# The sample's second SwiGLU on an unnormalised residual held in accumulators, and single banks for the last down products

## The chip, the core and the metric

The kernel runs on one core of one Trainium2 chip. A core has five engines that run on their own and wait for each other by semaphores: TensorE (PE in the profile, its weight loads PEld), VectorE (DVE), ScalarE (ACT), GpSimd (POOL) and SyncE (SP), which here issues nearly all DMAs. The metric is the device time of one launch in microseconds; lower is better. The time before is a median of 2969.23 us.

## What is computed

A two-layer encoder trunk with a residual stream of width 1024, for two request groups with the same weights: a prompt of 1024 tokens and a sample of 512. Layer 0 mixes tokens by a grouped Fourier transform, layer 1 by grouped-query attention; after each comes a dense SwiGLU with 2816 hidden columns.

```python
def rms_norm(x, g):
    y = xf * lax.rsqrt(jnp.mean(xf * xf, axis=-1, keepdims=True) + EPS)
    return (y * g.astype(jnp.float32)).astype(x.dtype)

def swiglu_ffn(x, g, w_gate, w_up, w_down):
    h = rms_norm(x, g)
    return (jax.nn.silu(h @ w_gate) * (h @ w_up)) @ w_down

for i in range(DEPTH):
    x = x + (fourier_mixer if i % 2 == 0 else attention_mixer)(x, ...)
    x = x + swiglu_ffn(x, norm_ffn[i], ...)
```

Since the norm's factor `rsqrt(mean(x*x) + EPS)` is one number per token, `(r*x*g) @ w` equals `r * ((x*g) @ w)`: the factor may be put on a product's result.

## The kernel before

Tokens lie along the free dimension in blocks of 512: block 0 is the sample, blocks 1 and 2 are the prompt. A residual is eight tiles of 128 features by 512 tokens. Every float32 operand is split into a high and a low part (`split`, L238: ACT writes the high part, DVE or POOL the low one), and every product is three matmuls (`mm3`, L249 to L251).

Two streams are written as Python generators and interleaved by `weave`. Each `yield` states an estimated cost, and the stream with the least stated cost so far goes on. A scheduler then sets each engine's order; a later instruction can be put ahead where it does not depend on what stands before. Each engine executes in its order and waits at the head.

The sample's stream, `main_1`, is attention's projections (`qkv(0)`), its attention, the output projection (`out_projection`, `linear_residual`), `prepare`, and the second SwiGLU (`ffn(1, 0, ...)`). It runs beside `aux_2`, the prompt's projections, attention, output projection and the preparation (`moving`) of the prompt's second SwiGLU. That one (`ffn_pair`) follows alone and fills the last 600 us; it treats the prompt's two blocks together by a scheme with seven products for eight.

Around the change:
- `linear_residual` loads the old residual into a temporary `x`, adds the product, and gives it to `new_residual`. That stores it to DRAM (`xres`, L332), squares it, and sums the squares in `ss`. After the last tile `rstd_cols` (L308) sums over features on PE, and `rsqrt` makes the factor on DVE.
- `prepare(0, 1)` runs `normed`: `in_rows` (L316, L317) spreads the factor over the partitions on PE, each residual tile is reloaded (L366), multiplied by it (L369) and by the gain, and split into `h` (L245, L246).
- `ffn` goes through 22 chunks of 128 hidden columns. A chunk has a gate chain and an up chain of 24 matmuls each into two banks `ga`, `up` (tiles `g`, of which there are two), then Silu (L851), product (L852) and split. The down products (`c<-mid`) of two chunks are added to eight accumulators. The accumulators are 4 buffers in all, two for a block, and attention's transposed tiles (`pt`) rotate through those that are free. For the sample's first SwiGLU (`here`) the residual already stands in accumulators, and the factor `first["r"]` is multiplied onto `ga` and `up` (L849, L850); for its second the accumulators are loaded from `xres`.
- `attend` treats 128 query rows at a time: `scores` (tile `g` or `a`, row maxima L1346, Exp L1350, scaling L1352), `turned` (transposes L1364, split into `pt`), and after each second block `values`. The prompt's scores have one buffer of two banks.
- `product` in `ffn_pair` is one down product: three matmuls into `chain[d]` and a DVE add to an accumulator (L1054). A chain of products sums in its bank, and each partial sum is added to an accumulator. In all rounds but the last the four chains have single banks (tiles `c` and `g`); in the last they share two tiles of two banks each (`a`, of the pool that also takes the pair's gate and up sums). The output of a finished tile is sent at L329.

Of the kernel before, what the change touches and what calls it, by code (L numbers as in the profile page):

```python
# [10 lines left out]
F32 = mybir.dt.float32  # L11
# [3 lines left out]
ALU = mybir.AluOpType  # L15
# [4 lines left out]
NC = D // P  # L20
TB = 512
# [5 lines left out]
NF = DFF // P  # L27
# [98 lines left out]
def trunk_kernel(ctx: ExitStack, tc: tile.TileContext, t: dict):  # L126
# [59 lines left out]
    def tmp(n=TB, dt=F32):  # L186
        return tl("t", [n], dt, "t" + cur[0])
# [66 lines left out]
    nxt, first = {}, {}  # L254
# [71 lines left out]
    def new_residual(b, dc, piece, out=None, stays=False, room=None, later=None, ends=(0, NC - 1)):  # L326

        if out is not None:
            sp.dma_start(out, piece)  # L329
            return  # L330
        if not stays:
            sp.dma_start(xres[b][:, dc, :], piece)  # L332
        if dc == ends[0]:
            ss[b] = later if later is not None else room() if room else tl("ss", [TB], F32, "ss" + cur[0])
            act.activation(ss[b], piece, AF.Square)
        else:
            sq = room() if room else side()
            act.activation(sq, piece, AF.Square)
            dve.tensor_tensor(ss[b], sq, ss[b], op=ALU.add)
        if dc == ends[1]:  # L340
            rstd[b] = cp.tile([P, 4], F32, name=nm("rs"))
            if later is not None:
                whole_sums.append(b)
            else:
                rstd_cols(rstd[b], ss.pop(b), D)
# [398 lines left out]
    def linear_residual(src, u, b, prev):  # L744

        for n in range(NC):
            w = weights(src[n])
            x = tmp()
            sp.dma_start(x, prev[:, n, :])
            ps = bank()  # L750
            project(w, u, ps)
            dve.tensor_tensor(x, ps, x, op=ALU.add)
            new_residual(b, n, x)
            yield 5.5


    kept, pend = {}, []

    def ffn(layer, b, h, out=None):
        h = h()  # L760
        here = b in resident
        acc = resident.pop(b) if here else accumulators()
        kept[b] = acc
        yield 0.0

        def halves(ms, wds, f0, dc):

            box = []

            def half(i):  # L770
                w = wds[dc // 4].rearrange("p h (f c) n -> p h f c n", f=2)
                mm3(box[0], w[:, 0, i, dc % 4], w[:, 1, i, dc % 4], ms[i][:, 0], ms[i][:, 1], i == 0, i == 1)

            def begin():
                box.append(bank())
                if f0 == 0 and not here:
                    sp.dma_start(acc[dc], xres[b][:, dc, :])
                half(0)

            def end():  # L780
                half(1)
                dve.tensor_tensor(acc[dc], box[0], acc[dc], op=ALU.add)  # L782
                if f0 + 2 == NF:
                    new_residual(b, dc, acc[dc], None if out is None else out[:, dc, :])

            return begin, end

        def one(n=1):
            for _ in range(n):
                if pend:  # L790
                    pend.pop(0)()

        ready = {v: first[i] for i, v in enumerate((("gate", 0), ("up", 0), ("gate", 1)))} if here else {}

        def want(v, fc):
            if fc < NF and (v, fc) not in ready:
                ready[v, fc] = weights(down_src(layer, fc, "AB".index(v)) if v in "AB" else t[v][layer, fc])

        def open_items(ms, f0):

            wds = [ready.pop(("A", f0))]
            pairs = [halves(ms, wds, f0, dc) for dc in range(NC)]
            turns = [pairs[0][0], pairs[1][0], pairs[0][1], pairs[1][1]]
            for v in pairs[2:]:
                turns.extend(v)
            pend.extend(turns)
            return wds

        wds = None
        want("gate", 0)  # L810
        want("up", 0)
        for fc in range(NF):
            f0, odd_ = fc - fc % 2, fc % 2
            wg, wu = ready.pop(("gate", fc)), ready.pop(("up", fc))
            if not odd_ and wds is not None:
                want("B", f0 - 2)
                wds.append(ready.pop(("B", f0 - 2)))
            ga, up = bankg(), bankg()
            for dc in range(NC):
                if odd_ and dc == 4:  # L820
                    want("A", f0)
                part(wg, h, ga, dc)
                if here and fc == 0:
                    part(wu, h, up, dc)
                if not odd_ and dc >= 5:
                    one()
                if dc % 2:
                    yield 1.36 if odd_ or dc < 5 else 2.0 if dc == 5 else 2.7
            if odd_:
                want("gate", fc + 1)  # L830
                wds = open_items(ms, f0)
            for dc in range(NC):
                if not odd_ and dc == 3:
                    want("gate", fc + 1)
                if fc == NF - 1 and dc == 4:
                    want("B", f0)
                if dc == (2 if odd_ else 4):
                    want("up", fc + 1)
                if not (here and fc == 0):
                    part(wu, h, up, dc)  # L840
                if not odd_:
                    one(2 if dc in (2, 4, 6) else 1)
                elif dc >= 6:
                    one()
                if dc % 2:
                    yield (3.4 if dc > 1 else 2.7) if not odd_ else 2.7 if dc == 7 else 1.36
            s = tmp()
            if here:
                dve.tensor_tensor(ga, ga, first["r"], op=ALU.mult)  # L849
                dve.tensor_tensor(up, up, first["r"], op=ALU.mult)  # L850
            act.activation(s, ga, AF.Silu)  # L851
            dve.tensor_tensor(up, up, s, op=ALU.mult)  # L852
            m = tl("mid", [2, TB], F32R, "mid")
            split(m[:, 0], m[:, 1], up)
            if odd_:
                ms.append(m)
            else:
                ms = [m]
        want("B", NF - 2)
        wds.append(ready.pop(("B", NF - 2)))  # L860
# [61 lines left out]
    def ffn_pair(layer, blocks, ring, places, outs):  # L922
# [111 lines left out]
        def product(k, d, f0):  # L1034

            name, m, (o, c) = CHAINS[k]
            if f0 == 0 and d == 0 and k < 3:
                load_acc(*((blocks[1], 0), (blocks[1], 1), (blocks[0], 1))[k])
            if d == 0 and k % 2 == 0 and k < 6:
                next(preps[0])  # L1040
            if k == 6 and d == 3:
                preps.pop(0)
            b, dc = blocks[c], 4 * o + d
            acc = accs[b][dc]
            fresh, closes = k in (0, 4, 6), k in (3, 5, 6)
            if fresh and f0 + 2 < NF:
                chain[d] = bank() if d % 2 else bankg()
            elif fresh and d % 2 == 0:
                g2 = tl("a", [2, TB], F32, "gT", gt)
                chain[d], chain[d + 1] = g2[:, 0], g2[:, 1]  # L1050
            x, wd = spots[m], ops[name][:, :, d * P : (d + 1) * P]
            read[m] -= 1
            mm3(chain[d], wd[:, 0], wd[:, 1], x[:, 0], x[:, 1], fresh, True, skip_group_check=True)
            dve.tensor_tensor(acc, chain[d], acc, op=ALU.add)  # L1054
            if f0 + 2 == NF and LAST[o, c] == name:
                new_residual(b, dc, acc, None if outs is None else outs[b][:, dc, :], room=spare, later=sums_of(b, dc), ends=(4, 3))
# [248 lines left out]
    def attend(blocks, straight, slot):  # L1305
# [6 lines left out]
        for g in range(NKV):  # L1312
# [15 lines left out]
            for h in range(g * GROUP, (g + 1) * GROUP):  # L1328
# [49 lines left out]
                    act.copy(o, po[:, 0:256])  # L1378
                    sp.dma_start(dot[blocks[n]][:, h, c0 : c0 + 256], o)

                last = None
                for qc in range(nk + 1):
                    p = scores(qc) if qc < nk else None
                    yield 0.7 * nb
                    if qc:
                        turned(qc - 1, last)
                        yield 0.8 * nb
                        if qc % 2 == 0:
                            values(qc // 2 - 1)
                            yield 0.8 * nb  # L1390
                    last = p


    def weave(main, main_cost, aux=None, aux_cost=1.0, lead=0):
# [11 lines left out]
                runs.remove(run)  # L1406
        cur[0] = "F"

    FFN_US, PAIR_US, CHAIN_US, PROMPT_US = 352.0, 678.0, 223.0, 630.0

    mpt = open_pool("mp")
# [60 lines left out]

    def prepare(b, layer):

        yield from normed(b, g_ffn[layer], nxt, "A")

    def h_next():
        return nxt["h"]
# [62 lines left out]
    def main_1():  # L1541
        yield from qkv(0)
        yield from attend((0,), 0, "A")
        yield from out_projection(0, "A")
        yield from prepare(0, 1)
        yield from ffn(1, 0, h_next, t["y"][0])
# [128 lines left out]
```

## Time and profile before

| what | us |
|---|---|
| median of three runs (2968.76 to 2973.36) | 2969.23 |
| the profiled execution | 2965.4 |
| its span, from first to last instruction | 2963.6 |
| PE busy in the span | 2855.9 |
| DVE busy | 1713.3 |
| ACT busy | 1304.9 |
| POOL busy | 1517.6 |

A row of the profile names line, engine, operation, and output and inputs by the program's names. `a<-w,w` is the prompt's scores, `c<-ident,p` transposes of its probabilities, `c<-pt,w` its values, `c<-h,w` a projection, `g<-h,w` gate or up of the sample, `c<-mid,w` its down products, `a<-ring,w` and `a<-late,w` gate and up of the prompt's pair. A wait is put down to the instruction that ended last. A row such as "PE a L249 <- ACT p L1350: 6.1, 3, 2.5" says who waited, for whom, us in total, how often, and the longest.

### The profile page before, as it was taken

What the parts mean: (1) busy time and instruction counts of PE and PEld (TensorE: products, weight loads), DVE (VectorE), ACT (ScalarE), POOL (GpSimd) and SP (SyncE); (2) the same over time, 40 slices, a digit from 0 to 9 for tenths busy, and PEclk for the clock granted to TensorE, in tenths of its full rate; (3) what the DMA queues carried; (4) which work ended last, traced back from release to release, by engine and by line L of the source; (5) the groups of instructions that cost most, each with busy time, mean ns of one, the idle gap of its engine ahead of it and who ended that gap; (6) DMA issues with size and microseconds to landing.
All of it is one profiled execution on the core that took longest, in us unless ns stands there. A gap on an engine that the chain in (4) does not pass through costs nothing. (4 is left out here: it accounts for less than half of the span.)

```text
span 2963.6 us, 37198 instructions
## 1 busy us (share of the span) xinstructions
PE 2855.9 (96%) x13656; PEld 2350.0 (79%) x13656; DVE 1713.3 (58%) x3031; ACT 1304.9 (44%) x2131; POOL 1517.6 (51%) x932
## 2 busy tenths in 40 slices
PE   7999999999999999998998999999998999999998
PEld 6778878788888887786777888878886788888886
DVE  6674553566666667737646555552244466666666
ACT  5543232333333333646756776663333333333332
POOL 4344264766776774522241122224535767766763
PEclk8999999999999999999999999999999999999999
DMA  7435374766556553632242121115447865565552
GB/s 227 143 116 183 131 270 167 291 218 222 192 186 219 199 175 130 213 93 85 83 150 89 59 91 54 54 57 192 151 168 278 309 235 200 176 219 201 192 195 89
DMA packets 182326, 496.82 MB, mean 168 GB/s; under 512 B 19872, under 2 KB 30112, under 8 KB 180736
## 3 DMA queue, kind: packets, MB, share of 16 engines
q1 hardware_dynamic: 181216, 489.65, 48.5%
q0 software_dynamic: 640, 3.74, 0.4%
q8 instruction: 108, 1.77, 0.2%
q10 hardware_dynamic: 288, 1.05, 0.1%
q14 instruction: 74, 0.61, 0.1%
HBM read 426.21 MB, written 68.16 MB: 167 GB/s over the span
## 5 line engine op out<-in xcount | busy, mean ns | idle before, releaser
L288 POOL TENSOR_TENSOR w<-raw,w 128x1024 fp32r<-128x1024 f32 x200 | 479.0, 2402 | 843.9 <-ACT w L287 832.7
L243 POOL TENSOR_TENSOR w<-raw,w 128x512 fp32r<-128x512 f32 (+1 forms) x464 | 608.3, 1331 | 451.2 <-ACT w L242 445.0
L242 ACT CAST w<-raw 128x512 fp32r<-128x512 f32 (+1 forms) x464 | 279.6, 632 | 538.3 <-PE a L251 173.2
L287 ACT CAST w<-raw 128x1024 fp32r<-128x1024 f32 x200 | 208.7, 1049 | 269.5 <-PE g L251 77.9
L249 PE MATMUL g<-h,w 128*128 128x512 f32 x704 | 279.3, 397 | 9.9 <-ACT w L287 3.4
L251 PE MATMUL g<-h,w 128*128 128x512 f32 x704 | 277.8, 395 | 2.2 <-POOL w L288 2.2
L249 PE MATMUL a<-ring,w 128*128 128x512 f32 x712 | 279.5, 392 | 0.1
L251 PE MATMUL a<-ring,w 128*128 128x512 f32 x712 | 277.5, 390 | 0.0
L250 PE MATMUL a<-ring,w 128*128 128x512 f32 x712 | 277.3, 389 | 0.0
L250 PE MATMUL g<-h,w 128*128 128x512 f32 x704 | 276.8, 393 | 0.0
L1054 DVE TENSOR_TENSOR acc<-g,acc 128x512 f32<-128x512 f32 x280 | 192.5, 687 | 106.9 <-PE g L251 106.6
L1054 DVE TENSOR_TENSOR acc<-c,acc 128x512 f32<-128x512 f32 x280 | 192.4, 687 | 93.7 <-PE c L251 92.1
L249 PE MATMUL c<-mid,w 128*128 128x512 f32 x592 | 232.4, 393 | 13.3 <-ACT mid L242 7.6
L250 PE MATMUL c<-mid,w 128*128 128x512 f32 x592 | 232.6, 393 | 1.2 <-DVE mid L243 1.1
L251 PE MATMUL c<-mid,w 128*128 128x512 f32 x592 | 232.5, 393 | 1.3 <-POOL w L288 1.3
L249 PE MATMUL c<-h,w 128*128 128x512 f32 x480 | 191.5, 400 | 4.3 <-ACT h L245 3.3
L782 DVE TENSOR_TENSOR acc<-c,acc 128x512 f32<-128x512 f32 x176 | 120.9, 688 | 129.2 <-PE c L251 126.5
L250 PE MATMUL c<-h,w 128*128 128x512 f32 x480 | 189.1, 395 | 1.2 <-DVE h L246 0.9
L251 PE MATMUL c<-h,w 128*128 128x512 f32 x480 | 188.9, 394 | 0.0
L249 PEld LDWEIGHTS g<-h,w 128*128 128x128 f32 x704 | 133.0, 189 | 37.1 <-ACT w L287 3.8
L249 PEld LDWEIGHTS a<-ring,w 128*128 128x128 f32 x712 | 133.8, 188 | 33.8 <-DVE mid L243 4.4
L251 PEld LDWEIGHTS g<-h,w 128*128 128x128 f32 x704 | 132.9, 189 | 30.0 <-POOL w L288 3.3
(392 smaller groups left out, 6718.5 us busy)
## 6 DMA issues: line engine op xcount, KB each, us to landing
ring<-mov_B SPq DMA_DIRECT2D x248, 512.0 KB, 5.5
ring<-mov_T SPq DMA_DIRECT2D x88, 512.0 KB, 5.1
raw<-in_gate_dram SPq DMA_DIRECT2D x44, 512.0 KB, 3.6
raw<-in_up_dram SPq DMA_DIRECT2D x44, 512.0 KB, 3.5
raw<-in_down_dram SPq DMA_DIRECT2D x88, 256.0 KB, 3.1
raw<-in_gate_dram SPq DMA_DIRECT2D x88, 256.0 KB, 5.0
raw<-in_up_dram SPq DMA_DIRECT2D x88, 256.0 KB, 5.4
raw<-in_down_dram SPq DMA_DIRECT2D x44, 512.0 KB, 4.1
```

The lines of the kernel that those rows point to most:

```text
L242: keep(act.copy(hi, src))
L243: keep(eng.tensor_tensor(lo, src, hi.bitcast(F32), op=ALU.subtract))
L249: pe.matmul(out, lh, rh, start=first, stop=False, **kw)
L250: pe.matmul(out, lh, rl, start=False, stop=False, **kw)
L251: pe.matmul(out, ll, rh, start=False, stop=last, **kw)
L287: pinned(act.copy(flat[:, 0], raw)) if early else act.copy(flat[:, 0], raw)
L288: pool.tensor_tensor(flat[:, 1], raw, flat[:, 0].bitcast(F32), op=ALU.subtract)
L782: dve.tensor_tensor(acc[dc], box[0], acc[dc], op=ALU.add)
L1054: dve.tensor_tensor(acc, chain[d], acc, op=ALU.add)
```

## The change

The sample's residual after attention stays in accumulators (`staying[0]`, taken before the output projection), with no store and no reloads. `prepare` splits it times the gain alone. The sum over features and the `rsqrt` (`settled`) are called in chunk 0 of the SwiGLU, the row broadcast after that chunk's up chain, and the factor is multiplied onto `ga` and `up` in each chunk of this SwiGLU too. In `product` the last round of layer 1 (`outs is not None`) takes single banks. The loop of `attend` states other costs at its yields, with the same operations in the same sequence within the stream. The profile's lines after L752 move on by a few.

```diff
         for n in range(NC):
             w = weights(src[n])
-            x = tmp()
+            x = staying[b][n] if b in staying else tmp()
             sp.dma_start(x, prev[:, n, :])
...
-            new_residual(b, n, x)
+            new_residual(b, n, x, stays=b in staying, later=(tl("ss", [TB], F32, "ssF") if n == 0 else ss[b]) if b in staying else None)
...
-        acc = resident.pop(b) if here else accumulators()
+        acc = resident.pop(b) if here else staying[b]
...
-                if f0 == 0 and not here:
-                    sp.dma_start(acc[dc], xres[b][:, dc, :])
...
+                if fc == 0 and not here and dc == 1:
+                    settled(b)
...
-            if here:
-                dve.tensor_tensor(ga, ga, first["r"], op=ALU.mult)
-                dve.tensor_tensor(up, up, first["r"], op=ALU.mult)
+            if fc == 0 and not here:
+                first["r"] = tl("ss", [TB], F32, "ssF")
+                act.copy(first["r"], in_rows(rstd[b]))
+            dve.tensor_tensor(ga, ga, first["r"], op=ALU.mult)
+            dve.tensor_tensor(up, up, first["r"], op=ALU.mult)
...
-            if fresh and f0 + 2 < NF:
+            if fresh and (f0 + 2 < NF or outs is not None):
                 chain[d] = bank() if d % 2 else bankg()
...
-                last = None
-                for qc in range(nk + 1):
-                    p = scores(qc) if qc < nk else None
-                    yield 0.7 * nb
-                    if qc:
-                        turned(qc - 1, last)
-                        yield 0.8 * nb
-                        if qc % 2 == 0:
-                            values(qc // 2 - 1)
-                            yield 0.8 * nb
-                    last = p
+                ps = []
+                for qc in range(nk + LAG):
+                    if qc < nk:
+                        ps.append(scores(qc))
+                        yield 0.7 * nb
+                    n = qc - LAG
+                    if n >= 0:
+                        turned(n, ps[n])
+                        yield (0.2 if n % 2 else 2.0) * nb
+                        if n % 2:
+                            values(n // 2)
+                            yield 0.2 * nb
...
+    LAG = 1
...
     def prepare(b, layer):
-        yield from normed(b, g_ffn[layer], nxt, "A")
+        h = h_tile("A")
+        for dc in range(NC):
+            split(h[:, 0, dc], h[:, 1, dc], staying[b][dc], gain=g_ffn[layer][:, dc : dc + 1])
+        nxt["h"] = h
+        yield 1.0
...
         yield from attend((0,), 0, "A")
+        staying[0] = accumulators()
         yield from out_projection(0, "A")
```

PE before, from the output projection's last matmul (`c_13204<-h_10881`) on; scores, transposes and the norm's sum (L308) follow:

```order
L251 MATMUL c_13204<-h_10881,w_13199 128x512
L249 MATMUL a_13253<-w_12614,w_13178 128x512
...
L1364 MATMUL c_13271<-ident,p_13193 128x128 x4
L1364 MATMUL c_13278<-ident,p_13193 128x128 x4
L308 MATMUL c_13235<-ones,ss_12494 128x1 x4
...
L249 MATMUL g_13537<-h_13371,w_13529 128x512
```

Between the norm's sum and the gate's first matmul (`g_13537<-h_13371`, the last row) stand 85 rows, of attention and of the broadcast. PE after, from the same last matmul (`c_13127<-h_10881`) on:

```order
L251 MATMUL c_13127<-h_10881,w_13123 128x512
L249 MATMUL a_13205<-w_12647,w_13202 128x512
L250 MATMUL a_13205<-w_12647,w_13202 128x512
L1366 MATMUL c_13157<-ident,p_13101 128x128 x4
L1366 MATMUL c_13164<-ident,p_13101 128x128 x4
...
L249 MATMUL g_13280<-h_13237,w_13272 128x512
...
L249 MATMUL c_13171<-pt_13105,w_12648 128x256
```

The gate's first matmul has moved to the ninth row behind the projection, and the norm's sum stands 65 rows behind it. DVE before, in the last round of the pair; `a_23742` and `a_23751` are tiles of two banks, each of which carries two of the four chains:

```order
L1054 TENSOR_TENSOR acc_18663<-a_23751,acc_18663 128x512
L1054 TENSOR_TENSOR acc_18666<-a_23742,acc_18666 128x512
L1054 TENSOR_TENSOR acc_18663<-a_23751,acc_18663 128x512
L1054 TENSOR_TENSOR acc_18664<-a_23742,acc_18664 128x512
L1054 TENSOR_TENSOR acc_18665<-a_23751,acc_18665 128x512
```

DVE after, in the same round, beside the last instructions of the pair's gate and up values (`mid_18688`, `ring_18145`):

```order
L243 TENSOR_TENSOR mid_18688<-a_23692,mid_18688 128x512
L1056 TENSOR_TENSOR acc_18681<-c_23747,acc_18681 128x512
L1056 TENSOR_TENSOR acc_18682<-g_23732,acc_18682 128x512
L243 TENSOR_TENSOR ring_18145<-a_23692,ring_18145 128x512
L1056 TENSOR_TENSOR acc_18682<-c_23737,acc_18682 128x512
L1056 TENSOR_TENSOR acc_18682<-g_23742,acc_18682 128x512
L1056 TENSOR_TENSOR acc_18682<-c_23747,acc_18682 128x512
```

The adds read four tiles of one bank each, `g_23732`, `c_23737`, `g_23742` and `c_23747`, one after the other. By count the change leaves PE with the same 13390 instructions, gives DVE 36 more, ACT one more copy and two more table loads, and takes 24 DMAs from SP's queue.

More of the change, by code (lines that the diff above doesn't have):

```diff
@@ L752, in linear_residual @@
             dve.tensor_tensor(x, ps, x, op=ALU.add)
-            new_residual(b, n, x)
+            new_residual(b, n, x, stays=b in staying, later=(tl("ss", [TB], F32, "ssF") if n == 0 else ss[b]) if b in staying else None)
             yield 5.5
-    kept, pend = {}, []
+    kept, pend, staying = {}, [], {}
     def ffn(layer, b, h, out=None):
```

## The prediction

> **What bounds the kernel now.** I read the page's busy line first, then its slices, then windows of busy time by stage.
>
> ```profile
> span 2963.6 us, 37198 instructions
> PE 2855.9 (96%) x13656; PEld 2350.0 (79%) x13656; DVE 1713.3 (58%) x3031; ACT 1304.9 (44%) x2131; POOL 1517.6 (51%) x932
> ...
> 1340.00:1500.00 160.00, 146.23 (x804) 118.13 (x803) 106.40 (x248) 112.18 (x213) 37.89 (x21) 1.00 0.25 80
> 1601.46:1636.19 34.73, 25.09 (x136) 21.41 (x134) 24.93 (x57) 23.05 (x38) 2.35 (x1) 0.85 0.22 68
> 1636.19:2030.00 393.81, 380.41 (x2147) 320.75 (x2148) 210.45 (x383) 263.74 (x369) 102.75 (x43) 1.00 0.23 75
> 2200.00:2312.00 112.00, 99.81 (x410) 79.46 (x409) 47.41 (x72) 36.18 (x53) 65.23 (x38) 0.94 0.78 277
> 2312.00:2923.00 611.00, 610.11 (x2679) 500.86 (x2677) 388.30 (x592) 219.19 (x394) 436.94 (x308) 1.00 0.60 207
> 2929.10:2963.60 34.50, 26.39 (x84) 15.58 (x84) 23.07 (x34) 2.39 (x4) 2.53 (x3) 0.89 0.33 122
> ```
>
> The columns of a window are its length, the busy time and count of PE, weight loads, DVE, ACT and POOL, then granted clock, DMA share and GB/s. PE is the bound: in the pair stage (2312 to 2923) it is busy 610 of 611 us, and nothing that this change touches can shorten that. The change can win only where PE waits. Two such stretches lie on its lines: 1601 to 1636, between the sample's output projection and its second SwiGLU, and the last 34.5 us. In both the granted clock is also low (0.85 and 0.89).
>
> Busy time overstates PE, because matmuls overlap. The rate is read from starts:
>
> ```profile
> 1601.46 0.39 PE L249 MATMUL a<-w,w 128*128 128x512 f32 x1
> 1601.69 0.39 PE L250 MATMUL a<-w,w 128*128 128x512 f32 x1
> ...
> 1602.82 1.03 PE L1364 MATMUL c<-ident,p 128*128 128x128 f32 x8
> ...
> 1607.92 0.63 PE L251 MATMUL a<-w,w 128*128 128x512 f32 x1
> 1608.35 0.63 PE L249 MATMUL a<-w,w 128*128 128x512 f32 x1
> ```
>
> A 512-column matmul takes 0.227 us of PE at full clock and 0.43 us after a wait has halved the clock; a transpose pass takes about 0.11 us (1.03 for eight, the last one's tail included).
>
> **Term 1: the gap before the second SwiGLU.** The output projection's last matmul is followed at 1601.46 by prompt attention alone, until the gate's first matmul:
>
> ```profile
> 1636.19 0.50 PE L249 MATMUL g<-h,w 128*128 128x512 f32 x1 [2.10 <-DVE h L246]
> ...
> PE a L249 <- ACT p L1350: 6.1, 3, 2.5
> PE g L249 <- DVE h L246: 2.1, 1, 2.1
> PE c L249 <- DVE pt L243: 0.9, 1, 0.9
> ...
> L1364 PE MATMUL c<-ident,p 128*128 128x128 f32 x40 | 6.7, 318 | 0.0
> L249 PE MATMUL c<-pt,w 128*128 128x256 f32 x16 | 5.3, 329 | 0.9 <-DVE pt L243 0.9
> L249 PE MATMUL a<-w,w 128*128 128x512 f32 x10 | 4.8, 478 | 6.1 <-ACT p L1350 6.1
> ```
>
> Work in these 34.7 us: 30 score matmuls (three lines of 10) at 0.227 = 6.8; 48 value matmuls of half the columns, at half of that, 5.4; 40 transpose passes at 0.107 = 4.3; 16 small passes for the norm (8 on L308, 8 on L317), 1.7. That is 18.2 us, so 16.5 us are lost: waits for Exp, since one score buffer feeds the next block only after it, and half clock. The attention has nothing else to fill them, since the gate waits for sum of squares, rsqrt, row broadcast, eight row products and eight splits.
>
> After the change the order puts the gate's first matmuls six score matmuls and eight transposes behind the projection. What remains late:
> - h. The last residual's add, then two splits on DVE stand ahead of the gate's second chunk: 0.69 + 2 x 0.75 = 2.2 us, against 6 x 0.227 + 0.9 = 2.2 us of PE work. I take 0.3 us. The values that come next wait for two DVE subtractions behind those splits, about 0.9 us (the row above for the same wait).
> - The row scale at the end of chunk 0. The broadcast's copy (0.6), the gate's product (0.69), a table load (1.28) and Silu (0.6) stand between the broadcast and the next gate chain on the same bank; six score matmuls (1.4) cover part: 1.8 us, up to 3 if an Exp is ahead.
> - Attention itself: the order shows one block whose transposes stand only some 15 matmuls behind its scores, 1.5 to 2 us short.
>
> ```profile
> L246 DVE SCALAR_TENSOR_TENSOR h<-g,gains,h 128x512 fp32r<-128x512 f32 x8 | 5.7, 746 | 1.0 <-ACT h L245 1.0
> L369 DVE TENSOR_TENSOR g<-c,t 128x512 f32<-128x512 f32 x8 | 5.4, 692 | 0.2 <-PE c L317 0.2
> L752 DVE TENSOR_TENSOR t<-c,t 128x512 f32<-128x512 f32 x1 | 0.7, 692 | 4.2 <-PE c L251 4.2
> ```
>
> About 5 us stay (2 to 9): -11.5 us (-14.5 to -7.5).
>
> **Term 2: the last down products.** 28 products of three matmuls, each followed by a DVE add, run at the end with two banks in one tile:
>
> ```profile
> 2929.11 0.50 PE L249 MATMUL a<-mid,w 128*128 128x512 f32 x1
> ...
> 2944.61 0.50 PE L249 MATMUL a<-mid,w 128*128 128x512 f32 x1
> 2945.42 0.42 PE L249 MATMUL a<-mid,w 128*128 128x512 f32 x1
> 2945.62 1.41 DVE L1054 TENSOR_TENSOR acc<-a,acc 128x512 f32<-128x512 f32 x2 [0.33 <-PE a L251]
> 2946.36 0.50 PE L249 MATMUL a<-mid,w 128*128 128x512 f32 x1
> ...
> 2959.62 0.69 DVE L1054 TENSOR_TENSOR acc<-a,acc 128x512 f32<-128x512 f32 x1 [0.36 <-PE a L251]
> ```
>
> Two products take 1.75 us (2944.61 to 2946.36) where six matmuls are 1.36: a product starts only when the add on the tile's other bank is done. On four single banks the same products in the stage before run at the matmul rate, and the adds follow 0.60 us apart:
>
> ```profile
> 2912.37 0.68 DVE L1054 TENSOR_TENSOR acc<-c,acc 128x512 f32<-128x512 f32 x1
> 2912.97 0.68 DVE L1054 TENSOR_TENSOR acc<-g,acc 128x512 f32<-128x512 f32 x1
> ```
>
> New tail: the order moves two products ahead of the last gate and up product, into a wait there; 26 x 0.68 = 17.7 us follow 2929.1. Ten of them lead to the operand N4, at 2935.9; it needs 13 DVE instructions of 0.69 from 2929.1, so 2938.1: a wait of 2.2. PE ends at 2949.0, the last add at 2949.9 against 2960.3: -10.4.
>
> ```profile
> GB/s 0 0 0 0 0 0 0 0 0 0 0 0 14 348 0 234 127 76 285 0 305 57 147 215 356 356 226 359 206 291 147 381 393 294 367 260 342 23 0 0
> out_y_dram<-acc SPq DMA_DIRECT2D x16, 256.0 KB, 2.0
> ```
>
> The outputs would then leave at 0.26 MB per 0.7 us, 375 GB/s, near the highest of these slices (2935 to 2964; one transfer lands in 2.0 us), so the last may land 1 us later: -9.5 us. Bounds: -5 if the adds keep their 0.88 us apiece (26 x 0.88 = 22.9), -12.5 without the wait for N4.
>
> **Term 3: 44 row products more, 8 fewer, on DVE.** The first SwiGLU of the sample does the same already:
>
> ```profile
> L849 DVE TENSOR_TENSOR g<-g,ss x22: 680/700/700, 109.6 to 528.9; 128x512 f32<-128x512 f32 x22
> ...
>   ACT t L851: 5.8, 3
> ```
>
> 44 x 0.69 = 30 us, over some 660 us (1636 to 2300) in which DVE is about half busy. They hold a gate or up bank 0.7 us longer, but that bank is wanted one chain (24 x 0.227 = 5.4 us) later. In the first SwiGLU only ACT waits for them. Behind them in DVE's queue stand attention's maxima, for which Exp and then PE wait: some 20 of the 44 fall before 2030, 14 us of DVE. If a third shows on PE, +4. The attention's new cost figures move the other way: transposes stand a few matmuls farther behind their scores, and PE idles 13.4 us in that stretch. I take both together as 0 (-8 to +8); the cover is other matmuls, and without it each costs its 0.69 us.
>
> **Small parts.** 24 transfers leave SP's queue: 8 stores, 8 reloads for the norm, 8 for accumulators; 8 loads go to accumulators instead of temporaries, the last four behind up's first weight load, some 5 us before use.
>
> ```profile
> SPq L332 <- DVE t L752: 14.9, 3, 9.2
> SPq L366 <- DVE col L1347: 17.0, 2, 13.0
> ...
> L851 ACT ACT_TABLE_LOAD x11 | 14.1, 1283 | 0.2
> ```
>
> SP stood 32 us at these stores and reloads with weight loads behind it, but no PE wait of the gap names a weight: 0. Attention's transposed tiles now share two accumulator buffers already during the projection, as they do later anyway: 0 (to +2). Two table loads are added, Silu and Exp alternating more: 2 x 1.28, half behind matmuls, +1.3.
>
> The Trainium skill, page "ScalarE: Activation LUTs", section "What ACT_TABLE_LOAD costs", speaks against the change: it puts a switch at about 2.66 us, 1.28 for the load and 1.38 for a drain. By that rule, an estimate from the page, the two loads would cost 2.7 in place of 1.3. The trace shows the 1.283 and, with 0.2 us idle ahead of eleven loads, no drain.
>
> The stage at 2200 to 2312 prepares the prompt's operands, with the sample's SwiGLU as cover; the order leaves 403 gate, up and down matmuls behind that stage's broadcast where 428 were. 0, from -3 to +5.
>
> **Sum** against the profiled execution, 2965.4 us (span 2963.6 and 1.8 around it): -11.5 - 9.5 + 0 + 1.3 + 0 = -19.7, so 2945.7. That execution is 3.8 under the median of the runs shown, 2969.2; on the median's footing I forecast 2949.5 us.
>
> **Rivals.**
> - A. The gap's gain is given back at 2200 to 2312: that stage has DMA at 0.78 and waits for ACT and POOL, so a sample that is ahead leaves it with less cover. For it: 12 us of PE idle there now. Against: only 25 matmuls fewer remain. Tail alone: 2959.7.
> - B. The tail stays bound by DVE, because the N4 operand's instructions and adds share it. Gap and loads alone: 2959.0.
> - Both A and B: about 2969, no change.
> - C. The row products reach PE: 44 x 0.69 = 30.4 on its path, at the bank of each chunk. It decides above 19.7 / 44 = 0.45 us apiece. Against it stands that only ACT waits for L849. Price: 2979.9, slower.
> - D. The farther transposes also win the 13.4 us of idle after 1636: 2936.
>
> By the Trainium skill, "TensorE: Matmul & The Clock Gate", section "What's actually happening", the clock halves after an idle window of about 3.4 us. Here it halved behind waits of at most 2.5 us, so the trace disagrees, and I keep half-clock time within what stays of the gap.
>
> **Chances.** Forecast 0.56, D 0.07, A 0.13, B 0.11, A and B 0.08, C 0.05. What a measurement of this kernel can tell from no change is about 0.2%, 6 us. Faster 0.87, same 0.08, slower 0.05. The range 2937 to 2962 holds the forecast with its bounds, A and B.
>
> **What would show it.** Gap: the gate's first matmul within 3 us of the projection's last, and no run of waits on Exp beside it. Tail: products 0.7 us apart, the last add about 21 us after the N4 product. It is wrong if waits on row products appear at gate chains, or if 2200 to 2312 grows by the 11 us won.

## The result, and the profile after

The changed kernel took 2941.57 us, the median of four runs (2939.29 to 2943.94), beside 2968.99 for the kernel before (2966.21 to 2973.36): ratio 0.9906, 95% interval 0.9889 to 0.9924, 27.4 us on the medians. The forecast was 2949.5. The profiled execution, 2943.94 with a span of 2942.2, lies above its median, and that of before under its own, so the two traces differ by 21.5 us.

The busy line of the page, then windows: the 34.7 us behind the projection, and the stretch from the last gate or up matmul of the pair to the end (columns as in the prediction).

```profile
PE 2851.2 (97%) x13656; PEld 2350.9 (80%) x13656; DVE 1737.2 (59%) x3067; ACT 1307.7 (44%) x2134; POOL 1516.2 (52%) x932
...
1595.69:1630.40 34.71, 33.34 (x202) 28.24 (x202) 24.39 (x56) 28.28 (x45) 6.96 (x3) 1.00 0.15 50
2915.64:2942.20 26.56, 19.41 (x80) 14.17 (x78) 20.34 (x33) 2.88 (x6) 3.34 (x3) 0.94 0.42 159
```

PE runs the same 13656 matmuls. The first window held 136 of them before and holds 202 now, at a clock of 1.00 where it was 0.85. The same end in the kernel before:

```profile
2928.70:2963.60 34.90, 26.79 (x86) 15.58 (x84) 23.43 (x35) 2.54 (x5) 2.93 (x3) 0.89 0.32 121
```

34.90 us became 26.56, so 8.3 less.

PE's timeline at the gap, then who waited for whom in the 50 us from 1595.46:

```profile
1595.46 0.39 PE L251 MATMUL c<-h,w 128*128 128x512 f32 x1
1596.57 0.50 PE L249 MATMUL a<-w,w 128*128 128x512 f32 x1 [0.72 <-ACT p L1352]
1596.90 0.40 PE L250 MATMUL a<-w,w 128*128 128x512 f32 x1
1597.95 1.09 PE L1366 MATMUL c<-ident,p 128*128 128x128 f32 x8 [0.65 <-ACT p L1354]
...
1599.81 0.39 PE L249 MATMUL g<-h,w 128*128 128x512 f32 x1
...
PE a L249 <- ACT p L1352: 2.8, 2, 2.1
PE c L1366 <- ACT p L1354: 0.6, 1, 0.6
PE g L249 <- ACT t L853: 0.2, 1, 0.2
```

The gate starts 4.35 us behind the start of the projection's last matmul, without a wait of its own; it was 34.96. The waits for Exp fell from 6.1 to 2.8. The longest one left, 2.1 us, stands where the row scale is made. ACT and PE there, behind the row broadcast's last matmuls (L317, 1632.82):

```profile
1633.55 0.60 ACT L850 COPY ss<-c 128x512 f32<-128x512 f32 x1
1634.20 1.20 ACT L1352 ACTIVATE p<-a,col,rqc 128x1024 f32<-128x1024 f32 x1
...
1635.51 1.28 ACT L853 ACT_TABLE_LOAD   x1
1636.81 0.60 ACT L853 ACTIVATE t<-g 128x512 f32<-128x512 f32 x1
```

```profile
1635.55 0.50 PE L249 MATMUL a<-w,w 128*128 128x512 f32 x1 [2.11 <-ACT p L1352]
...
1637.46 0.49 PE L249 MATMUL g<-h,w 128*128 128x512 f32 x1 [0.25 <-ACT t L853]
```

The copy of the row factor, an Exp, the table load and Silu follow each other on ACT. PE waits 2.1 us for that Exp, runs six score matmuls, and waits another 0.2 us for Silu before the next gate chain.

The tail: PE and DVE at the first products, at the operand N4 (in `ring`), and at the last add:

```profile
2915.64 0.39 PE L251 MATMUL a<-late,w 128*128 128x512 f32 x1
2915.87 0.39 PE L249 MATMUL g<-mid,w 128*128 128x512 f32 x1
...
2916.55 0.39 PE L249 MATMUL c<-mid,w 128*128 128x512 f32 x1
...
2920.49 0.47 PE L249 MATMUL g<-mid,w 128*128 128x512 f32 x1 [0.32 <-DVE acc L1056]
...
2921.60 0.50 PE L249 MATMUL c<-mid,w 128*128 128x512 f32 x1 [0.17 <-DVE acc L1056]
...
2922.66 0.68 DVE L1056 TENSOR_TENSOR acc<-c,acc 128x512 f32<-128x512 f32 x1
2923.26 0.68 DVE L1056 TENSOR_TENSOR acc<-g,acc 128x512 f32<-128x512 f32 x1
2923.85 0.68 DVE L243 TENSOR_TENSOR ring<-a,ring 128x512 fp32r<-128x512 f32 x1
2924.20 0.40 PE L249 MATMUL g<-ring,w 128*128 128x512 f32 x1
...
2927.44 0.68 DVE L1056 TENSOR_TENSOR acc<-g,acc 128x512 f32<-128x512 f32 x1
2928.04 0.68 DVE L1056 TENSOR_TENSOR acc<-c,acc 128x512 f32<-128x512 f32 x1
...
2935.72 0.69 DVE L1056 TENSOR_TENSOR acc<-c,acc 128x512 f32<-128x512 f32 x1
```

Where it does not wait, a product now follows the one before by 0.68 us (2915.87 to 2916.55), the matmul rate, against 0.88. From 2916.07 to the end of the last add DVE is never idle: its 33 instructions are busy 20.34 us. Up to 2931 they start 0.60 us apart, the last adds 0.68 us, and two products wait for an add. So the new tail is held by DVE as much as by the matmuls. The last add ends 20.8 us behind the start of the pair's last gate or up matmul, and the span ends 5.8 us later. Before, these were 31.6 (2928.70 to 2960.31) and 3.3: the adds won 10.8, and the outputs took 2.5 of it back. Their landing, in the row of the outputs over the last 8 us, of after and of before:

```profile
out_y_dram<-acc SPq DMA_DIRECT2D x5, 256.0 KB, 4.1
```

```profile
out_y_dram<-acc SPq DMA_DIRECT2D x7, 256.0 KB, 2.8
```

The row products on the gate (44 now, durations as minimum, median and maximum, then who waited for them):

```profile
L851 DVE TENSOR_TENSOR g<-g,ss x44: 672/698/700, 113.5 to 2279.2; 128x512 f32<-128x512 f32 x44
...
  ACT t L853: 20.3, 7
```

No PE wait names them.

### The profile page after: what moved, and what is told of

Its sections match the earlier page's. It is cut to its first block, busy times and chain, and to the rows that moved or that the text cites. A ratio compares the mean times of both kernels' runs of the same rounds, so it can differ in the third digit from the quotient of the medians.

```text
span 2942.2 us, 37189 instructions
## 1 busy us (share of the span) xinstructions
PE 2851.2 (97%) x13656; PEld 2350.9 (80%) x13656; DVE 1737.2 (59%) x3067; ACT 1307.7 (44%) x2134; POOL 1516.2 (52%) x932
## 4 chain that ended last, share of the span: by engine, by line
PE 42%; issue 3%; DVE 3%; POOL 2%; ACT 2%; DMA 2%; SPq 0%; POOLq 0%; DVEq 0%; ACTq 0%
PE a L249 6%; PE a L251 6%; PE a L250 6%; PE c L249 5%; PE c L250 4%; PE c L251 4%; PE g L251 3%; PE g L249 3%; PE g L250 3%; PE c L1366 2%; POOL w L288 1%; DVE col L1349 1%; DMA x<-xres 1%; DVE col L1348 1%; DVE acc L1056 1%
## 5 line engine op out<-in xcount | busy, mean ns | idle before, releaser
L288 POOL TENSOR_TENSOR w<-raw,w 128x1024 fp32r<-128x1024 f32 x200 | 479.2, 2403 | 852.0 <-ACT w L287 828.9
L287 ACT CAST w<-raw 128x1024 fp32r<-128x1024 f32 x200 | 208.3, 1048 | 280.6 <-PE g L251 97.0
L1056 DVE TENSOR_TENSOR acc<-g,acc 128x512 f32<-128x512 f32 x294 | 201.7, 686 | 105.2 <-PE g L251 104.9
L1056 DVE TENSOR_TENSOR acc<-c,acc 128x512 f32<-128x512 f32 x294 | 201.6, 686 | 93.2 <-PE c L251 91.5
L249 PE MATMUL c<-mid,w 128*128 128x512 f32 x604 | 237.4, 394 | 13.5 <-ACT mid L242 9.5
L250 PE MATMUL c<-mid,w 128*128 128x512 f32 x604 | 236.7, 392 | 1.3 <-DVE mid L243 1.1
L251 PE MATMUL c<-mid,w 128*128 128x512 f32 x604 | 236.4, 392 | 0.0
L780 DVE TENSOR_TENSOR acc<-c,acc 128x512 f32<-128x512 f32 x176 | 120.8, 688 | 112.6 <-PE c L251 111.9
```

The lines of the kernel that those rows point to most:

```text
L249: pe.matmul(out, lh, rh, start=first, stop=False, **kw)
L250: pe.matmul(out, lh, rl, start=False, stop=False, **kw)
L251: pe.matmul(out, ll, rh, start=False, stop=last, **kw)
L287: pinned(act.copy(flat[:, 0], raw)) if early else act.copy(flat[:, 0], raw)
L288: pool.tensor_tensor(flat[:, 1], raw, flat[:, 0].bitcast(F32), op=ALU.subtract)
```

## Where the waits went

For the rest I use a tally of my own: from the start of each matmul to the next, less its pitch (0.227 us for 512 columns, 0.12 for 256, 0.06 for 128), gaps under 0.06 left out, summed by stage. "Attention" is the sample's attention and projection, "gap" the 35 us from the projection's last matmul, "middle" from there to the prompt attention's last values, "operands" from the last row broadcast to the first matmul of the pair on `late`. The whole stretch, from the sample's first score to that matmul, holds 4854 or so matmuls in every kernel, so its length compares them. One profiled execution of each kernel is compared; the two traces of the changed kernel agree within 0.9 us in every stage.

| kernel (profiled execution) | attention | gap | middle | operands | length |
|---|---|---|---|---|---|
| before | 40.0 | 17.2 | 26.0 | 19.4 | 994.9 |
| changed (first trace) | 35.2 | 3.3 | 24.6 | 21.0 | 977.8 |
| changed (e4) | 34.3 | 3.3 | 24.6 | 20.3 | 976.2 |
| residual alone (e3) | 40.0 | 5.4 | 29.4 | 27.3 | 996.4 |
| residual alone, 5.0 stated (e10) | 41.9 | 5.3 | 20.1 | 20.5 | 981.8 |
| figures alone (e2) | 34.6 | 14.0 | 27.2 | 22.1 | 991.0 |
| figures alone, weight 619 (e11) | 37.9 | 15.4 | 23.4 | 20.1 | 991.0 |
| before, weight 625 (e9) | 42.7 | 16.9 | 27.9 | 21.0 | 1000.6 |
| without row products (e5) | 34.1 | 3.3 | 26.6 | 20.7 | 979.0 |
| changed, weight 660 (e7) | 39.4 | 2.8 | 27.6 | 15.1 | 979.0 |
| changed, 9.0 stated (e8) | 35.0 | 3.3 | 26.6 | 23.0 | 981.6 |
| changed, weight 680 (e12) | 40.4 | 6.0 | 27.6 | 17.2 | 984.9 |

Where the gap ends is a choice, and it matters. In the kernels with the late norm, waits around the row broadcast and the row scale fall in the 15 us behind the 35 (3.2 us in the changed kernel's first trace, 4.5 with the residual alone, 0.2 before) and count as "middle". With a gap of 50 us, as in the first expectation under the second heading below, the gap is 17.5 before, 6.5 in the changed kernel and 9.9 with the residual alone, and the middle 25.7, 21.5 and 24.8.

Two windows' rows of this stretch, of before and of e4, show the same from the busy time:

```profile
1347.45:2342.34 994.89, 938.41 (x4854) 777.27 (x4854) 491.71 (x952) 550.54 (x843) 342.34 (x169) 0.99 0.37 125
```

```profile
1346.57:2322.77 976.20, 934.87 (x4855) 774.17 (x4854) 513.81 (x988) 553.55 (x846) 342.80 (x169) 0.99 0.36 120
```

## The experiments

Kernels under one heading ran on the same chip beside the same runs of before, whose medians were 2967.97, 2968.63 and 2966.38 us in the three groups. Differences in us are of medians. The ratios in brackets, with their 95% intervals, are not the ratios of the medians and differ from these by up to 2.5 us.

### The three parts apart, and the whole

The last chains alone, on the kernel before:

```diff
-            if fresh and f0 + 2 < NF:
+            if fresh and (f0 + 2 < NF or outs is not None):
```

> The kernel before with the single banks of the last down chains alone. Theory (each of the three parts pays in its own place): 8 to 9.5 us less than before, all of it behind the first product of the last round; matmuls of that round 0.60 to 0.70 us apart per product instead of 0.875, and the last adds 0.6 to 0.7 us apart. Rival (the tail is VectorE's own rate, the gain of the whole lies elsewhere): under 3 us less.

2958.82 us, 9.2 less (ratio 0.9974, 0.9964 to 0.9985). From the pair's last matmul to the end:

```profile
2931.66:2957.60 25.94, 19.40 (x80) 14.17 (x78) 20.32 (x33) 2.88 (x5) 3.32 (x3) 0.94 0.43 162
```

That is the changed kernel's tail, 9.0 us shorter than before's 34.90, in a kernel that is otherwise the old one. The theory holds (by the ratio the gain is 7.7 us, just under its 8) and the rival's price falls. DVE is busy 20.32 of these 25.94 us, so its rate now limits this tail too, but with adds 0.60 to 0.69 us apart instead of 0.88.

The figures of attention's yields alone:

```diff
-                        yield 0.8 * nb
-                        if qc % 2 == 0:
-                            values(qc // 2 - 1)
-                            yield 0.8 * nb
...
+                        yield (0.2 if n % 2 else 2.0) * nb
+                        if n % 2:
+                            values(n // 2)
+                            yield 0.2 * nb
```

> The kernel before with only the new cost figures at attention's yields. Theory (the stretch of sample attention, 148.8 us before and 141.6 after, was shortened by the order of the blocks, and nothing in the residual part touches it): 5 to 9 us less than before, with the stretch from the sample attention's first to its last row of blocks 5 to 8 us shorter and the 35 us hole before the second SwiGLU still there with its stores and reloads. Rival 1 (the shorter attention stretch is where the residual part's moved work went, not the figures): within 2 us of before. Rival 2 (the figures bring something only together with the row products, since they move the transposes behind them): slower than before by 2 us or more.

2964.73 us, 3.2 less (0.9988, 0.9976 to 1.0000): under the theory's 5 to 9, and hardly told apart from no change. The stretch of the sample's attention did shrink, from 148.8 us to 141.8, so it was the figures that shortened it. But it also holds 22 matmuls less (727 for 749); the tally's waits in it fell by 3.9 us, from 26.1 to 22.2. Some of what PE waited for there, before and with the figures alone:

```profile
PE g L249 <- ACT t L1350: 4.1, 5, 1.1
PE g L251 <- POOL w L243: 2.4, 4, 0.6
PE c L250 <- DVE w L243: 1.8, 2, 1.2
```

```profile
PE g L251 <- POOL w L243: 2.1, 4, 0.6
PE c L1364 <- ACT t L1352: 1.9, 4, 0.7
...
PE g L249 <- ACT t L1350: 0.6, 1, 0.6
```

The waits of the scores for Exp (L1350) went from 4.1 to 0.6, while transposes now wait 1.9 us for their scaled block (none before). But middle and operands gave back 1.2 and 2.7 (26.0 to 27.2, 19.4 to 22.1).

The residual part alone (the changed kernel with the old loop in `attend` and the old condition in `product`):

```diff
-            if fresh and (f0 + 2 < NF or outs is not None):
+            if fresh and f0 + 2 < NF:
...
-                        yield (0.2 if n % 2 else 2.0) * nb
+                        yield 0.8 * nb
```

> The changed kernel with the old two-bank last chains and the old cost figures at attention's yields, so the residual in accumulators, the late norm and the row products alone. Theory: 10 to 13 us less than before, of that 11 from the gap ahead of the second SwiGLU (gate's first matmul within 5 us of the projection's last start), and the 44 row products cost 0 to 2 us. Rival 1 (the row products delay attention's transposes, and the new cost figures only make up for that): 4 to 8 us less. Rival 2 (the residual part brings all that the tail does not): 17 to 20 us less.

2965.30 us, 2.7 less (0.9994, 0.9985 to 1.0003). The theory had 10 to 13, and even the first rival 4 to 8; by its interval this kernel is not told apart from before. The gap was closed (17.2 to 5.4), and 11.3 us came back: 3.4 in the middle and 7.9 with the operands. With a gap of 50 us it wins 7.6 only (17.5 to 9.9), the middle gives nothing back, and the 7.9 stay. This is rival A of the prediction, in a kernel with one part of the change. The longest of PE's waits in the stage with the operands, before, here, and in the whole (e4):

```profile
PE g L249 <- ACT w L287: 3.4, 1, 3.4
PE c L249 <- ACT w L287: 2.6, 1, 2.6
PE c L249 <- ACT mid L242: 2.5, 2, 2.3
```

```profile
PE c L249 <- ACT w L287: 6.8, 1, 6.8
PE c L251 <- POOL w L288: 3.7, 2, 2.4
PE c L249 <- ACT mid L242: 3.2, 2, 2.3
```

```profile
PE g L249 <- ACT w L287: 6.4, 1, 6.4
PE c L249 <- ACT mid L242: 4.7, 3, 3.2
```

All of PE's rows in that stage add up to 12.2, 18.4 and 12.3 us. PE waits there largely for the SwiGLU's weights, which ACT (L287) and POOL (L288) turn into operands while they make the pair's as well. ACT itself waits in that stage for the weights' transfers, and SP, which issues them, stands at the stores of the pair's operands (L905) until POOL has made them. Both are so in the kernel before too (8.6 us in two waits for up's transfers, 23.7 at the stores). The rows of ACT and SP with the residual part alone:

```profile
ACT w L287 <- DMA raw<-in_gate_dram: 5.5, 1, 5.5
ACT w L287 <- DMA raw<-in_down_dram: 4.5, 1, 4.5
...
SPq L283 <- POOL w L288: 23.6, 5, 7.2
SPq L905 <- POOL l L243: 22.0, 12, 4.4
```

SP's longest row is at the weight loads themselves (L283), which wait until POOL has read the buffer: 23.6 us here, 18.1 before and 14.5 in e4. I take it that what differs is where PE's order meets these waits; no run shows that by itself.

The changed kernel itself:

> The changed kernel itself, beside the three parts on the same chip. Theory: 25 to 29 us less than before, and the three parts' differences add up to it within 3 us. Rival (the parts hang together): the sum of the three misses it by more than 5 us.

2941.66 us, 26.3 less (0.9914, 0.9899 to 0.9929). The parts alone add up to 15.1, so the parts hang together by 11 us, and the rival holds. The 11.3 us that the residual part gave back by itself (7.9 with a gap of 50 us) are of that size, which suggests where the difference lies and does not prove it.

### What it hangs on: row products, and the stated costs

The residual part alone with `prepare` stating 9.0 us:

```diff
         nxt["h"] = h
-        yield 1.0
+        yield 9.0
```

> The residual part alone as in the run before, but the sample's split of the residual states 9.0 us to the weave instead of 1.0, as the old normalisation there stated; no instruction is added or taken away. The residual part alone won 7.6 us of TensorE's waits at the gap (17.5 us of them between 1600 and 1650 before, 9.9 with it) and had 8.0 us more between 2150 and 2350 (28.4 against 20.4), where the pair's moving operands are made beside what is left of the sample's SwiGLU: 547 matmuls there against 578. Theory (the gain is given back there because the main stream states 8 us less and so runs ahead): 6 to 12 us less than before, and the waits of that stage back within 3 us of before's. Rival 1 (the row products cost it): within 3 us of the residual part alone. Rival 2 (the stage is held by its transfers, 0.79 of the DMA time, whatever stands beside it): within 3 us of the residual part alone, with waits of 25 us or more there.

2958.40 us, 10.2 less (0.9957, 0.9944 to 0.9971), 7.5 more than with 1.0. The theory's 6 to 12 holds. So a good part of the residual part's loss is one of order and not of its work; both rivals fall. The profiled execution took 2972.6, 14 us over the median of its runs, so I read no stage from it, and what the theory says of that stage's waits stays open.

The changed kernel without 42 of the 44 row products:

```diff
+            if here or fc == 0:
-            dve.tensor_tensor(ga, ga, first["r"], op=ALU.mult)
-            dve.tensor_tensor(up, up, first["r"], op=ALU.mult)
+                dve.tensor_tensor(ga, ga, first["r"], op=ALU.mult)
+                dve.tensor_tensor(up, up, first["r"], op=ALU.mult)
```

> The changed kernel without the row products behind chunk 0 of the second SwiGLU (42 of 44 left out, so that its later chunks are not scaled). My sum put them at nothing, with bounds of 8 us on both sides. Theory (VectorE has room, 0.59 of the span busy): within 2.5 us of the changed kernel. Rival (they stand ahead of attention's reductions and splits on VectorE and delay blocks): 4 us or more less than the changed kernel.

2945.04 us (0.9916, 0.9902 to 0.9929), nothing less than the changed kernel's 2941.66 in the other group (3.4 more by the medians, 0.6 by the ratios). These 42 row products cost nothing that can be measured; rival C falls, and so does the thought that they delay attention.

The changed kernel with the prompt's chain weighed at 660 us in the weave:

```diff
-    FFN_US, PAIR_US, CHAIN_US, PROMPT_US = 352.0, 678.0, 223.0, 630.0
+    FFN_US, PAIR_US, CHAIN_US, PROMPT_US = 352.0, 678.0, 223.0, 660.0
```

> The changed kernel with the prompt's chain weighed at 660 us instead of 630 in the weave, so that the second stream runs ahead and more of the sample's SwiGLU (some 80 gate, up and down matmuls more, 18 us of TensorE) is left when the pair's moving operands are made; no other edit. Theory (TensorE lacks work in that stage): 3 to 8 us less than the changed kernel. Rival 1 (the stage is held by its transfers, which the SwiGLU's weights share): within 2 us. Rival 2 (the second stream's attention blocks, closer together, wait more on ScalarE): 3 us or more slower than the changed kernel.

2937.91 us (0.9893, 0.9879 to 0.9906), 3.7 under the changed kernel's 2941.66 in the other group. The waits with the operands did fall, 20.3 to 15.1, but those of attention and of the middle rose by 8, and the two profiled executions have the same span (2935.9 and 2935.6). The lowest median here, in the theory's 3 to 8, and not told apart from the changed kernel.

The changed kernel with the split stating 9.0:

> The changed kernel with the split of the residual stating 9.0 us instead of 1.0, the counterpart of the first run of this call. In its order 72 gate and up matmuls of the SwiGLU come behind the pair's first product, where the changed kernel has none, as before had 96. Theory (what counts is how much SwiGLU is left when the stage begins, some 4 us more here): 0 to 4 us less than the changed kernel. Rival (what counts is that all of it stands ahead of the pair's first product): 3 to 8 us slower than the changed kernel.

2944.55 us (0.9914, 0.9900 to 0.9928), 2.9 over the changed kernel, near the lower end of the rival's 3 to 8 and within what two groups can differ. The theory that more SwiGLU left is enough by itself gets no support: 281 gate and up matmuls were left against 260, and the waits with the operands were 23.0 against 20.3.

### One pattern of order for all

Four kernels with the same pattern behind the last row broadcast (260 gate and up matmuls, 132 of down, ahead of the pair's first product): the changed kernel, and these three. The edits are the weave's 630.0 (to 625.0 on the kernel before, 619.0 with the figures alone) and the `yield` of `prepare` (5.0 with the residual alone).

> The kernel before with the prompt's chain weighed at 625 us instead of 630 in the weave, and nothing else. TensorE's order then has the same pattern behind the second stream's last row broadcast as the changed kernel's: all 260 gate and up matmuls that are left, and 132 of down, ahead of the pair's first product (before: 174 and 96, with 96 and 90 behind it). Theory (the parts hang together because they shift this pattern; the changed kernel happens on a good one): 4 to 8 us less than before, without any of the three parts. Rival (the pattern matters little, and what the residual part or the new figures win is lost elsewhere when they stand alone): within 3 us of before.

2970.83 us, 4.4 more than before (1.0014, 1.0003 to 1.0026). The pattern by itself wins nothing, so the theory falls; the rival's 3 us are passed on the far side.

> The residual part alone (old cost figures at attention's yields, old last chains), with the split stating 5.0 us instead of 1.0, which gives the changed kernel's pattern in that stage, 260 and 132 ahead of the pair's first product and no gate or up matmul behind. With 9.0 us stated it took 10.2 us less than before, with 1.0 us 2.7. Theory (the pattern decides): 9 to 13 us less than before. Rival (a single fortunate order): 2 to 6 us less.

2950.09 us, 16.3 less (0.9946, 0.9933 to 0.9959), more than the 9 to 13 expected. The gap is at 5.3 as with 1.0 stated; middle and operands are 20.1 and 20.5, against 29.4 and 27.3. Since before at 625 us has the same pattern and gained nothing, the pattern alone does not decide, and the range of neither side holds. The whole stretch, with 1.0 and with 5.0:

```profile
1345.56:2341.96 996.40, 939.58 (x4854) 776.74 (x4854) 521.00 (x988) 554.78 (x846) 342.32 (x169) 0.98 0.35 117
```

```profile
1348.56:2330.32 981.76, 936.93 (x4854) 777.25 (x4853) 513.87 (x988) 555.58 (x846) 342.35 (x168) 0.98 0.35 119
```

The same 4854 matmuls and 988 DVE instructions take 14.6 us less by a stated figure.

> The new cost figures alone, with the prompt's chain weighed at 619 us, 11 less, since the new figures state 1.4 us less for each of the eight heads of the pair's attention; this too has the changed kernel's pattern of 260 and 132 ahead of the pair's first product. With 630 us they took 3.2 us less than before: 7 us less in the sample's attention, and the waits of the stage with the moving operands 2.7 us more. Theory: 6 to 10 us less than before. Rival (the figures' gain is given back by the pair's attention, not by the pattern): 2 to 4 us less.

2966.54 us, no change (1.0001, 0.9990 to 1.0012). The theory falls, and so does the rival's 2 to 4: with that weight the figures win less in the sample's attention (37.9, where 630 gave 34.6 and before has 40.0), while middle and operands get better (23.4 and 20.1).

The last run carried the weight further:

> The changed kernel with the prompt's chain weighed at 680 us: 356 gate and up matmuls of the SwiGLU are left for the stage with the moving operands, all ahead of the pair's first product (260 in the changed kernel, 326 with 660 us, which took 2937.9 us). Theory (more work left, fewer waits there): 2934 to 2938 us. Rival (the blocks of the pair's attention stand too close together without the SwiGLU between them, and wait on ScalarE): 2941 us or more.

2946.40 us, 20.0 less than before (0.9935, 0.9923 to 0.9947), 4.7 over the changed kernel: the rival's time. The operands' waits stayed low (17.2), attention's rose to 40.4, the middle's to 27.6, and the gap had 6.0. The rival's reason is not shown: from the sample's first score to the prompt's last values the pair's scores wait 9.4 us for Exp where e4 has 7.2, but its transposes wait 3.0 us for their scaled blocks where e4 has 5.0.

What stays open is which place of the order makes the middle 20.1 in one kernel and 29.4 in another. Shown is that stated figures alone move a kernel of the same instructions by up to 13.6 us on the medians (residual alone, 2.7 to 16.3 less). With the pattern held the same, the parts do add up: relative to before at 625, in ratios, residual -0.0068, figures -0.0013, tail alone (against before itself) -0.0026, together -0.0107, where the whole has -0.0100, each ratio with an interval of 0.0010 to 0.0015 to either side, so that the comparison is good to some 0.003, or 8 us. I take that for agreement and not for proof, since that is wide beside the 11 us in question and the orders differ elsewhere too.

## Why the prediction was right, step by step

- **Term 1, the gap, -11.5.** The mechanism was right, and so was its size. In the table's 35 us, 17.2 us of waits became 3.3, but the row scale lies just behind them: in 50 us, 17.5 became 6.5, so -11.0, and 6.5 stay where I had kept 5 (2 to 9). The row scale was costed at 1.8 us of PE waiting, up to 3 with an Exp ahead; an Exp was ahead, and PE waited 2.1 us for it and 0.2 for Silu. The values' and h's waits that I kept are not in the rows. With the residual part alone 9.9 stay in 50 us.
- **Term 2, the tail, -9.5.** 9.2 alone, 8.3 between the two traces. The last add was put 20.8 us behind the first product of the tail and ends 20.5 behind it (2915.87 to 2936.41). Inside it the reason was partly wrong. There is no wait of 2.2 us for N4 (its product starts 0.35 us behind the start of the operand's last split). Instead the first thirteen products take 2.0 us more than at the matmul rate, in late starts of which the rows name two waits for adds; DVE has no idle time there. That is rival B's reason, adds and operands sharing DVE, at 0.60 us apiece instead of the 0.88 in B's price; that 2.0 is close to 2.2 is luck. The clock lost nothing: it was granted in full (1.00) from 2915.64 to 2935.60, and the 0.94 of the tail's row comes from behind PE's last matmul. Before, it was 0.51 from 2936.00 to 2942.20, a loss that the prediction had named and not priced apart. The outputs also land 2.5 us later than before did, where I had allowed 1.
- **Term 3, row products and figures together, 0.** The row products are 0, as costed. The figures are not: they brought 3.2 us by themselves and about 5 us of the whole (40.0 to 34.3 or 35.2 in attention). This is the mis-sized term. Rival D expected a gain from the figures by transposes that stand farther behind their scores, in the 13.4 us behind 1636. There PE's idle time is 13.0 us still (1630.40 to 2020.00, 376.62 of 389.60 busy), of which some 3 are the row scale's. The gain lies ahead of the gap, in the sample's own attention, where I had not looked for it, and there it is the scores that wait less for Exp.
- **Stage of the operands, 0 (-3 to +5).** +0.9 and +1.6 in the two traces. I took 25 matmuls less of cover for a small thing. In e3 33 less went with 7.9 us more of waits, so rival A was nearer than its 0.13. That the whole escaped it is owed to the order that the three parts have together, which I did not see coming: as far as the prediction goes, luck.
- **Table loads, +1.3.** There are two more, still of 1.283 us; no run separates their cost.
- **Sum.** Between the two traces, in lengths: 4.2 us more ahead of the stretch, of which 3.5 before the pair's first product, in code that the change does not touch; 17.1 less in the stretch (where the waits of the tally fell by 18.5: -4.8, -13.9, -1.4 and +1.6); 0.2 and 8.3 less behind it: -21.4, as the spans have it, where the sum had -19.7. The medians were 7.9 us under the forecast; about 5 of that are attention's figures and 3.8 the gap and middle together (-15.3 for -11.5), with 1.6 (the operands) and about 1 (the tail) the other way. That is some 6; the rest is not accounted for.
- **What would show it.** The gate's first matmul was to come within 3 us of the projection's last and came 4.35 us behind it. Products are 0.68 us apart where they do not wait, as said. That the last add comes "about 21 us after the N4 product" does not follow from the prediction's own sum, which has 11.8 (2938.1 to 2949.9); measured are 12.2 (2924.20 to 2936.41).
- **What would make it wrong** did not occur: no gate chain waits long for a row product (0.2 us by way of Silu), and the operands' stage did not grow by 11 us; even in e3 its waits grew by 7.9.

## What to carry to other kernels

Where two streams are woven by stated costs, a part that removes a stall also shifts which stream is ahead, and what it wins can be lost in a later stage where the two streams then stand differently: look at that stage's waits, restate the costs, and only then judge the part. A part that is measured alone under old figures is measured with its shift (2.7 us or 16.3 here). Postponing a row factor behind the matmuls was free for 42 of 44 products, on a vector engine that is 0.59 busy and waits for those matmuls anyway; making the factor still cost PE 2.1 and 0.2 us of waiting, once.

## What the runs showed that was not expected

- 256 KB outputs issued 0.68 us apart land 4.1 us after issue, where at 0.88 us apart they took 2.8: a faster end of the arithmetic gave 2.5 us of 10.8 back.
- The time to the pair's first product in the first layer was 531.7 to 541.8 us over the fourteen traces. None of the edits touches that code, so differences of single traces under some 5 us say little here.
